# Expert stage of a two-layer decoder: TensorE kept in program order, the next expert's one-hots made on VectorE, one product for a slot's index and weight

## The chip, the cores and the metric

The kernel runs on one core of a Trainium2 chip. The metric is the device time of one execution in microseconds (us).

## What is computed

A trunk of two layers for 512 tokens of width 1024. Each layer mixes tokens by two attention branches and then applies a SwiGLU feed-forward, dense in layer 0 and with experts in layer 1. The change lies in the experts:

```python
def moe_swiglu(h, w_router, w_gu_e, w_dn_e):
    logits = (h @ w_router).astype(jnp.float32)
    top_val, top_idx = lax.top_k(logits, TOP_K)               # 2 of 8
    top_w = jax.nn.softmax(top_val, axis=-1)
    combine = jnp.sum(jax.nn.one_hot(top_idx, N_EXPERTS) * top_w[..., None], axis=-2)
    out = jnp.zeros_like(h)
    for e in range(N_EXPERTS):
        out = out + combine[..., e:e + 1] * swiglu(h, w_gu_e[e], w_dn_e[e])
    return out                                                # D_FF_EXPERT = 1408
```

## The kernel before

**Experts in positions.** Experts are worked on one after the other, at positions e = 0 to 7. Position 0 is always expert 0; the other seven are ranked by how many tokens chose them and taken in the order of the table `ORDER`. An expert takes up to 192 tokens (`CAP`) as slots: 128 rows in the main pass, 64 in an overflow pass that stands in `If` blocks (`over`, L1482) and runs only where more than 128 tokens chose the expert. In the profiled execution that is so at positions 0 and 4.

**Numbers.** A matmul in full precision is made of three on fp32r parts (high by high, high by low, low by high). A weight *piece* (704 KB for gate and up, less for down) is loaded raw by SyncE (`e_load`, L1441), cast to its high part by ScalarE (L1467), and its low part is the difference that VectorE takes (L1468); `e_split` (L1455) issues both. There are 25 pieces to an expert, 16 for gate and up and 9 for down. Eleven raw and nine split pieces can be in memory.

**The stage of one expert** (`expert_blocks`, L1551) is a generator that stops at points (u, k). For u = 0 to 3 it computes 352 columns of gate and of up, over k = 0 to 7 chunks of the width: six matmuls for each k (L1646, L1647), 48 to a u. The overflow rows' 32 matmuls of a u (L1626) use a stationary tile that holds 64 high rows beside 64 low rows; `ov_gu` folds the two halves (a ScalarE copy, a VectorE sum, L1548 and L1549), twice, and multiplies (L1590). For d = 0 to 2, named u = 4 to 6, three matmuls for each of k = 0 to 10 make the down product (L1680 to L1682). It needs the transposed activations `ah` and `al`, which come in groups by `tr` (transposes L1576, ScalarE copy L1580, VectorE difference L1581); the last group is needed from k = 8 of d = 0. `ov_tr` does the same for the overflow rows (L1597, L1600, L1601) and 66 matmuls (L1694, L1695) use its result at the end of d = 0.

**The next expert** is prepared meanwhile, at points that the constants P0, PA, PA1, PA2, PB, PB1 and PO name. `prep_a` (L1485) makes one-hots of the slots, four of 128 by 192, from each token's rank (`one_hots`, L1268); multiplies them with token numbers, 16 products of one column (`slots`, L1278, L1288), and with the three parts of the weights, 8 of three columns (`slot_weights`, L1298, L1306), reads index and weight off, and gathers the rows by an indirect DMA from GpSimd's queue (L1500). `prep_b` (L1517) transposes the gathered rows into `xh` and `xl`; `prep_over` (L1532) does so for overflow rows. `route_rest` (L1206) computes weights, ranks and weight columns during position 0.

**What sets the order.** ScalarE's instructions stand as the program is written. Those of TensorE, VectorE, GpSimd and SyncE are placed by the framework's scheduler at build time; a few are tied by `keep_in_program_order` or a manual dependence. Each engine then runs its own list in order. PSUM tiles come from small rings: two for `py` (all transposes and slot products), four for `pa` (main accumulators), two for `mm` (overflow accumulators).

Of the kernel before, what the change touches and what calls it, by code (L numbers as in the profile page):

```python
# [43 lines left out]
ER = 11  # L44
EA = 4
ORDER = (7, 3, 4, 5, 0, 6, 1, 2)
P0 = (0, 2), (0, 6), (1, 1)
OV, OV3, OT, OY = 5, 6, 8, (5, 8)
ER0 = 3
LA = 2  # L50
SN = (2, 4, 6, 8), (2, 4, 6, 8), (2, 4, 6, 8), (2, 4, 6), (7, 8, 9, 10), (1, 4, 8), (1, 4, 8)
TU, TE = 5, 6
TD = 5
PA, PA1, PA2, PB, PB1, PO = (1, 2), (2, 0), (2, 4), (4, 2), (4, 7), (5, 4)
FD = 3
PINH = ()
BK = 0, 1, 2, 3, 4, 5, 6, 7
# [19 lines left out]
class Trunk:  # L77
# [1128 lines left out]
    def route_rest(self):  # L1206

        nc, rp = self.nc, self.rp

        def over_e(a):  # L1210
            return a.unsqueeze(2).to_broadcast([P, NT, NE])

        e2, w1 = rp.tile([P, NT], F32, name="e2"), rp.tile([P, NT], F32, name="w1")
        nc.vector.tensor_sub(e2, self.m8[:, :, 1], self.m8[:, :, 0])
        nc.scalar.activation(e2, e2, AF.Exp)
        nc.vector.tensor_scalar_add(w1, e2, 1.0)
        nc.vector.reciprocal(w1, w1)
        nc.vector.tensor_mul(e2, w1, e2)
        nc.vector.tensor_sub(self.M, self.M, self.s1)
        nc.vector.tensor_tensor(self.s1, self.s1, over_e(w1), op=ALU.mult)  # L1220
        nc.vector.tensor_tensor(self.M, self.M, over_e(e2), op=ALU.mult)
        nc.vector.tensor_add(self.wt, self.s1, self.M)
        self.rank()
        self.cols = rp.tile([P, NT, NE, 3], BF16, name="cols")
        self.weight_cols(self.cols, self.wtr, rp.tile([P, NT, NE], F32, name="wrem"))

    def rank(self):
# [40 lines left out]
    def one_hots(self, n, pos, q):  # L1268

        oh = []  # L1270
        for t in range(NT):
            o = self.ex.tile([P, CAP], BF16, tag="oh", bufs=4, name=self.nm("oh"))[:, :n]
            i = q.tensor_scalar(o, self.iotas[:, :n], pos[:, t], None, op0=ALU.is_equal)
            self.tc.keep_in_program_order(i)
            oh.append(o)
        return oh

    def slots(self, n, oh):  # L1278

# [205 lines left out]
    def prep_a(self, e):  # L1485

        nc, ex = self.nc, self.ex
        o = ORDER[e]
        oh = self.one_hots(CAP, self.posr[:, :, o:o + 1] if e else self.pos[:, :, 0:1], nc.gpsimd if e else nc.vector)
        yield  # L1490
        sl, fin = self.slots(CAP, oh)
        self.sl = sl
        if e:
            wfin = self.slot_weights(oh, sl, self.cols[:, :, o], self.psl)
            yield
        fin()
        g = self.g = [ex.tile([P, D], F32, tag="xg0", bufs=1, name=self.nm("xg")), self.views[-1]]

        def get(j):
            nc.gpsimd.indirect_dma_start(out=g[j], out_offset=None, in_=self.hd[:, :],  # L1500
                                         in_offset=bass.IndirectOffsetOnAxis(ap=sl[j][2], axis=0))

        get(0)
        if e == 0:
            self.counts()
        self.ne[e] = nc.values_load(self.cnti[0:1, o:o + 1] if e else self.cnti[0:1, NE:], min_val=0, max_val=S)
        with self.over(e):
            get(1)
        if e == 0:
            yield  # L1510
            self.route_rest()
            yield
            wfin = self.slot_weights(oh, sl, self.cols[:, :, o])
            yield
        wfin()

    def prep_b(self):  # L1517

# [32 lines left out]
    def expert_blocks(self, e, sl, xs, xo):  # L1551
# [51 lines left out]
        def ov_y(d):  # L1603
            c = dcol(d)
            self.fold(yo[:, c], ops[d][:, :c.stop - c.start], yo[:, c])
            nc.vector.tensor_scalar_mul(yo[:, c], yo[:, c], sl[1][3])

        def evac_gu(u, pg, pu):
# [8 lines left out]
        last = None  # L1617
        for u in range(DFE // GC):
            ws = self.e_next(KD // GK)
            with self.over(e):  # L1620
                for k in range(KD):
                    hi, lo = ws[k // GK]
                    st, sp, kk = k == 0, k == KD - 1, k % GK
                    for w, s0, s1 in ((hi, st, False), (lo, False, sp)):
                        for g in range(2):
                            nc.tensor.matmul(og[g], xo[:, k], w[:, g, kk], start=s0, stop=s1)  # L1626
            if u:
                evac_gu(u - 1, *last)
            last = pg, pu = self.psa()[:, :GC], self.psa()[:, :GC]
            for k in range(KD):  # L1630
                yield u, k
                if (u, k) == (0, ER0) and self.rest:
                    self.rest()
                if k == OV and u < 3:
                    with self.over(e):
                        ov_gu(u)
                if k == TU:
                    trev = tr(u * GC // P)
# [12 lines left out]
        for d in range(ND):  # L1651
            if d == 0:
                dws.append(self.e_next(3))
            if d != 1:
                py = self.psa()
            pd, py = py[:, :dcol(d).stop - dcol(d).start], None
            for k in range(KE):
                yield 4 + d, k
                if d == 0 and k == TD:
                    tr(KE)()  # L1660
                if k in SN[4 + d]:
                    self.e_split()
                if d == 0 and k == OV3:
                    with self.over(e):
                        ov_gu(3)
                if d == 0 and k == OT:
                    with self.over(e):
                        ov_tr()
                if d and k == 1:
                    evac_y(d - 1, last)  # L1670
                if (4 + d, k) == OY:
                    with self.over(e):
                        for j in range(ND):
                            ov_y(j)
                        nc.gpsimd.indirect_dma_start(out=self.out[0],
                                                     out_offset=bass.IndirectOffsetOnAxis(ap=sl[1][2], axis=0),
                                                     in_=yo, in_offset=None, compute_op=ALU.add)
                hi, lo = dws[d][k // DK]
                kk = k % DK
                nc.tensor.matmul(pd, ah[:, k], hi[:, 0, kk], start=k == 0, stop=False)  # L1680
                nc.tensor.matmul(pd, ah[:, k], lo[:, 0, kk], start=False, stop=False)  # L1681
                nc.tensor.matmul(pd, al[:, k], hi[:, 0, kk], start=False, stop=k == KE - 1)  # L1682
            last = pd
            if d == 0:
                py = self.psa()
                dws += [self.e_next(3) for _ in range(ND - 1)]
                ops.append(self.psa())
                with self.over(e):
                    for j, ws in enumerate(dws):
# [15 lines left out]
    def moe(self):  # L1705
# [19 lines left out]
            self.e_load()  # L1725
        self.hold = False
        next(pb)
        xo = self.prep_over(0)
        self.e_splits(1 + LA)
        for e in range(NE):  # L1730
            sl = self.sl
            for u, k in self.expert_blocks(e, sl, self.xs, xo):
                if e == 0 and (u, k) in P0:
                    next(pa, None)
                if e + 1 == NE:
                    continue
                if (u, k) == PA:
                    pa = self.prep_a(e + 1)
                if (u, k) in (PA, PA1, PA2):
                    next(pa, None)  # L1740
                if (u, k) == PB:
                    pb = self.prep_b()
# [74 lines left out]
    def whole(self):  # L1817
# [14 lines left out]
        with order:  # L1832
# [15 lines left out]
                self.route()  # L1848
            with experts:
                self.moe_pools(experts)  # L1850
                self.moe()
                with tc.issue_after(self.last_dve.ins):
                    self.overflow_list()
        with ExitStack() as experts:
# [29 lines left out]
```

## Time and profile before

| | |
|---|---|
| median of 3 runs | 1703.38 us (1703.5, 1700.21, 1703.38) |
| profiled execution, its own time | 1699.52 us |
| its span | 1697.7 us |
| expert matmuls in it, first and last start | 1198.0 us, 1684.97 us after the span's start |
| position 0 / 4 (with overflow rows) | about 84 / 86 us |
| each other position | about 52 us |

Positions follow each other without a gap on TensorE. The span begins at the first instruction; times of rows are counted from there, and 1.8 us of the profiled execution's own time lie outside it. In a profile's row, `out<-in` are tiles by the program's names, and the bracket at a row's end says how long the engine was idle before it and what released it.

### The profile page before, as it was taken

The numbers are of one execution on the slowest core, as the hardware profiler recorded it, in microseconds if no ns is written. First come the engines' busy times: TensorE is split into PE (matmuls) and PEld (weight loads), VectorE is DVE, ScalarE is ACT, GpSimd is POOL, SyncE is SP. The second block draws the span as 40 slices with busy tenths as digits, with TensorE's granted clock in tenths as the row PEclk, the third lists the DMA queues.
The fourth block names the chain that finished last, engine by engine and source line by source line (L and its number), as shares of the span: only waits on it lengthen the run. The fifth ranks groups of instructions, "written<-read, shape, count | busy, mean of one in ns | idle before, by whom it ended". The sixth has DMA issues, their size and how long they took to land. (4 is left out here: it accounts for less than half of the span.)

```text
span 1697.7 us, 26160 instructions
## 1 busy us (share of the span) xinstructions
PE 1634.0 (96%) x9031; PEld 1425.7 (84%) x9031; DVE 1093.7 (64%) x1844; ACT 977.9 (58%) x1750; POOL 205.5 (12%) x315
## 2 busy tenths in 40 slices
PE   6999999999999999999999999998899999999996
PEld 6878987888888888888878987887889999999996
DVE  5588678666533332336588688655767878767984
ACT  5677589755322222324677589643656776656873
POOL 6122000001000000100122000102012201102200
PEclk9999999999999999999999999999899999999998
DMA  7334332235333332443433233352959899869993
GB/s 181 108 96 116 82 88 71 86 110 165 100 98 99 100 99 84 134 130 100 112 105 107 72 88 78 110 194 95 311 201 331 296 360 351 295 209 336 321 344 87
DMA packets 270840, 273.73 MB, mean 161 GB/s; under 512 B 11424, under 2 KB 259232, under 8 KB 270688
## 3 DMA queue, kind: packets, MB, share of 16 engines
q1 hardware_dynamic: 255936, 230.98, 43.2%
q0 software_dynamic: 12288, 37.40, 8.1%
q10 hardware_dynamic: 2464, 3.41, 0.6%
q8 instruction: 85, 1.39, 0.3%
q14 instruction: 67, 0.55, 0.1%
HBM read 250.21 MB, written 13.14 MB: 155 GB/s over the span
## 5 line engine op out<-in xcount | busy, mean ns | idle before, releaser
L320 PE MATMUL mm<-b,whi 128*128 128x512 f32 x1072 | 426.7, 398 | 3.6 <-DVE b L534 2.7
L322 PE MATMUL mm<-b,wlo 128*128 128x512 f32 x1072 | 419.4, 391 | 0.0
L321 PE MATMUL mm<-b,whi 128*128 128x512 f32 x1072 | 419.4, 391 | 0.0
L297 DVE TENSOR_TENSOR wlo<-wr,whi 128x1024 fp32r<-128x1024 f32 (+1 forms) x176 | 213.3, 1213 | 214.5 <-ACT whi L296 212.5
L296 ACT CAST whi<-wr 128x1024 fp32r<-128x1024 f32 (+1 forms) x176 | 183.2, 1043 | 268.9 <-PE mm L321 121.5
L1468 DVE TENSOR_TENSOR elo<-er,ehi 128x1408 fp32r<-128x1408 f32 (+3 forms) x200 | 305.1, 1569 | 26.0 <-ACT ehi L1467 15.9
L1467 ACT CAST ehi<-er 128x1408 fp32r<-128x1408 f32 (+3 forms) x200 | 256.2, 1324 | 18.7 <-DMA er<-in_w_gu_exp_dram 6.2
L320 PEld LDWEIGHTS mm<-b,whi 128*128 128x128 f32 x1072 | 201.7, 188 | 45.4 <-DVE b L534 4.7
L322 PEld LDWEIGHTS mm<-b,wlo 128*128 128x128 f32 x1072 | 201.3, 188 | 42.8 <-DVE wlo L297 0.4
L321 PEld LDWEIGHTS mm<-b,whi 128*128 128x128 f32 x1072 | 201.7, 188 | 38.5 <-issue 0.2
L356 PE MATMUL mm<-whi,b 128*128 128x256 f32 x320 | 92.0, 288 | 1.8 <-DVE b L532 1.1
L357 PE MATMUL mm<-wlo,b 128*128 128x256 f32 x320 | 91.0, 285 | 0.4 <-DVE wlo L297 0.4
L358 PE MATMUL mm<-whi,b 128*128 128x256 f32 x320 | 90.8, 284 | 0.0
L1681 PE MATMUL pa<-elo,ah 128*128 128x352 f32 (+1 forms) x264 | 85.6, 324 | 2.7
L1682 PE MATMUL pa<-ehi,al 128*128 128x352 f32 (+1 forms) x264 | 84.4, 320 | 3.3 <-DVE al L1581 3.3
L1680 PE MATMUL pa<-ehi,ah 128*128 128x352 f32 (+1 forms) x264 | 86.2, 327 | 0.9
L1647 PE MATMUL pa<-elo,xh 128*128 128x352 f32 x256 | 83.7, 327 | 2.1 <-PEq L1620 0.5
L1646 PE MATMUL pa<-ehi,xh 128*128 128x352 f32 x256 | 85.7, 335 | 0.0
L1647 PE MATMUL pa<-ehi,xl 128*128 128x352 f32 x256 | 83.2, 325 | 0.9
L1646 PE MATMUL pa<-elo,xh 128*128 128x352 f32 x256 | 83.0, 324 | 0.3 <-DVE elo L1468 0.3
L1646 PE MATMUL pa<-ehi,xl 128*128 128x352 f32 x256 | 83.2, 325 | 0.0
L1647 PE MATMUL pa<-ehi,xh 128*128 128x352 f32 x256 | 82.9, 324 | 0.0
(351 smaller groups left out, 3087.7 us busy)
## 6 DMA issues: line engine op xcount, KB each, us to landing
er<-in_w_gu_exp_dram SPq DMA_DIRECT2D x248, 352.0 KB
wr<-in_w_in_dram SPq DMA_DIRECT2D x80, 512.0 KB
wr<-in_w_gu_dense_dram SPq DMA_DIRECT2D x44, 512.0 KB
er<-in_w_dn_exp_dram SPq DMA_DIRECT2D x32, 704.0 KB
wr<-in_w_dn_dense_dram SPq DMA_DIRECT2D x20, 512.0 KB
er<-in_w_dn_exp_dram SPq DMA_DIRECT2D x16, 640.0 KB
er<-in_w_dn_exp_dram SPq DMA_DIRECT2D x16, 528.0 KB
b<-b POOLq DMA_DIRECT2D x64, 128.0 KB, 2.8
```

Of the source, the lines that this page charges most:

```text
L296: self.nc.scalar.copy(hi, raw)
L297: self.nc.vector.tensor_sub(lo, raw, f32v(hi))
L320: self.nc.tensor.matmul(ps, hi[:, j], hh[j], start=st, stop=False)
L321: self.nc.tensor.matmul(ps, hi[:, j], hl[j], start=False, stop=False)
L322: self.nc.tensor.matmul(ps, lo[:, j], hh[j], start=False, stop=sp)
L356: nc.tensor.matmul(o, a, hi[:, j], start=first, stop=False, skip_group_check=True)
L357: nc.tensor.matmul(o, a, lo[:, j], start=False, stop=False, skip_group_check=True)
L358: nc.tensor.matmul(o, b, hi[:, j], start=False, stop=last, skip_group_check=True)
L1467: self.nc.scalar.copy(hi, raw)
L1468: self.last_dve = self.nc.vector.tensor_sub(lo, raw, f32v(hi))
L1646: nc.tensor.matmul(pg, x[:, k], w[:, 0, kk], start=s0, stop=s1)
L1647: nc.tensor.matmul(pu, x[:, k], w[:, 1, kk], start=s0, stop=s1)
```

## The change

- `moe` is traced with TensorE in program order too, so a matmul stands where the generator issues it.
- The one-hots of positions 1 to 7 are made by VectorE, not GpSimd, and at an earlier point: (0, 6) in place of (1, 2), with the products at (1, 5) in place of (2, 0). In position 0 these points are later: (2, 1), (2, 6) and, for the gather, (3, 1).
- The weight columns get two more, the token numbers in two parts (`cols` has 5), copied there by GpSimd once; `slots_all` makes index and weight by one set of 8 products of five columns, in place of 16 and 8.
- In position 0 the overflow rows are prepared inside the loop, at (0, 2), and their first matmuls stand at (0, 4); `route_rest` stands ahead of the loop, the slots' weights at (2, 0) and (2, 2).
- `ov_gu` of the last piece stands at k = 5 of u = 3 like the others' (before: at k = 6 of d = 0), and `ov_tr` at k = 3 of d = 0 (before: 8). That of position 0's first piece stands at k = 7.

```diff
-P0 = (0, 2), (0, 6), (1, 1)
-OV, OV3, OT, OY = 5, 6, 8, (5, 8)
+P0 = (2, 0), (2, 2)
+EO = 2
+OV, OT, OY = 5, 3, (5, 8)
-PA, PA1, PA2, PB, PB1, PO = (1, 2), (2, 0), (2, 4), (4, 2), (4, 7), (5, 4)
+PA = ((2, 1), (2, 6), (3, 1)), ((0, 6), (1, 5), (2, 4))
+PB, PB1, PO = (4, 2), (4, 7), (5, 4)
...
+        self.cols = rp.tile([P, NT, NE, 5], BF16, name="cols")
+        for j in range(2):
+            nc.gpsimd.tensor_copy(self.cols[:, :, :, 3 + j], self.tokc[:, :, j:j + 1].to_broadcast([P, NT, NE]))
...
+    def slots_all(self, n, oh, cols):
...
+            o = ps[:m, (b // P) * 8:(b // P) * 8 + 5]
+            for t in range(NT):
+                nc.tensor.matmul(o, oh[t][:, b:b + m], cols[:, t], start=t == 0, stop=t == NT - 1)
...
+                    nc.vector.tensor_reduce(ix, o[:, 3:5], axis=AX.X, op=ALU.add)
+                nc.vector.tensor_reduce(w, o[:, 0:3], axis=AX.X, op=ALU.add)
...
-        oh = self.one_hots(CAP, self.posr[:, :, o:o + 1] if e else self.pos[:, :, 0:1], nc.gpsimd if e else nc.vector)
+        oh = self.one_hots(CAP, self.posr[:, :, o:o + 1] if e else self.pos[:, :, 0:1], nc.vector)
         yield
-        sl, fin = self.slots(CAP, oh)
+        sl, fin = self.slots_all(CAP, oh, self.cols[:, :, o]) if e else self.slots(CAP, oh)
...
         for u in range(DFE // GC):
             ws = self.e_next(KD // GK)
+            if (e, u) != (0, 0):
+                mm_over()
...
             for k in range(KD):
                 yield u, k
+                if (e, u, k) == (0, 0, EO):
+                    xo = self.prep_over(0)
+                    self.e_splits(LA)
+                if (e, u, k) == (0, 0, EO + 2):
+                    mm_over()
-                if k == OV and u < 3:
+                if k == (OV if e or u else KD - 1):
                     with self.over(e):
                         ov_gu(u)
...
-                if d == 0 and k == OV3:
-                    with self.over(e):
-                        ov_gu(3)
...
-        xo = self.prep_over(0)
-        self.e_splits(1 + LA)
+        xo = None
+        self.e_splits(1)
+        next(pa)
+        p0 = pa
...
-                self.moe()
+                with tc.manual_schedule(engines={mybir.EngineType.PE}):
+                    self.moe()
```

`mm_over` is the block of a u's 32 overflow matmuls, unchanged, now a function.

**What moves on the engines.** Ahead of the expert stage all lists are the same, but for the two copies on GpSimd. TensorE, the slot products for position 1, before (tile `oh` is a one-hot, `tokc` the token numbers, `mm` the overflow accumulators):

```order
L1288 LDWEIGHTS oh_12022
L1288 MATMUL py_12137<-tokc,oh_12022 128x1
L1620 COMPARE_AND_BRANCH
L1626 MATMUL mm_11660<-ehi_11945,aot 128x352
L1626 MATMUL mm_11661<-ehi_11945,aot 128x352
L1626 MATMUL mm_11660<-elo_11946,aot 128x352
L1626 MATMUL mm_11661<-elo_11946,aot 128x352
```

and now:

```order
L1289 LDWEIGHTS oh_12135
L1289 MATMUL py_12210<-cols,oh_12135 128x5
L1289 LDWEIGHTS oh_12137
L1289 MATMUL py_12210<-cols,oh_12137 128x5
L1289 LDWEIGHTS oh_12139
L1289 MATMUL py_12210<-cols,oh_12139 128x5
L1289 LDWEIGHTS oh_12141
L1289 MATMUL py_12210<-cols,oh_12141 128x5
```

Before, the 16 index products were cut by an overflow block and by main matmuls, and 8 weight products followed; now 8 products stand together, ahead of the block, and nothing follows them.

TensorE, the end of d = 0 in position 0, before (`ao` are overflow activations, `aot` their transposes, `al` the low part of the main ones):

```order
L1680 MATMUL pa_12399<-ehi_12337,ah_11801 128x352
L1681 MATMUL pa_12399<-elo_12338,ah_11801 128x352
L1667 COMPARE_AND_BRANCH
L1597 MATMUL py_12468<-ident,ao 128x64 x8
L1597 MATMUL py_12479<-ident,ao 128x64 x3
L1667 UNCONDITIONAL_BRANCH x2
L1682 MATMUL pa_12399<-ehi_12337,al_11802 128x352
L1688 COMPARE_AND_BRANCH
L1694 MATMUL mm_11660<-ehi_12260,aot 128x352
```

and now, nearer to the start of d = 0:

```order
L1696 COMPARE_AND_BRANCH
L1620 MATMUL py_12414<-ident,ao 128x64 x8
L1620 MATMUL py_12425<-ident,ao 128x64 x3
L1696 UNCONDITIONAL_BRANCH x2
L1709 MATMUL pa_12394<-ehi_12226,ah_11820 128x352
L1710 MATMUL pa_12394<-elo_12227,ah_11820 128x352
L1711 MATMUL pa_12394<-ehi_12226,al_11821 128x352
L1709 MATMUL pa_12394<-ehi_12247,ah_11820 128x352
L1710 MATMUL pa_12394<-elo_12248,ah_11820 128x352
L1711 MATMUL pa_12394<-ehi_12247,al_11821 128x352
L1599 MATMUL py_12437<-ident,am 128x128 x3
```

The overflow transposes stood one main matmul ahead of the first matmul that reads `aot`; now they stand behind 9 of the 33 main matmuls, and the last `am` transposes come behind them.

VectorE, the same place, before:

```order
L1529 TENSOR_TENSOR xl_12407<-py_12408,xh_12406 128x512
L1664 COMPARE_AND_BRANCH
L1549 TENSOR_TENSOR ao<-mm_11660,ao 64x352
L1549 TENSOR_TENSOR ao<-mm_11661,ao 64x352
L1590 TENSOR_TENSOR ao<-ao 64x352
L1664 UNCONDITIONAL_BRANCH x2
L1581 TENSOR_TENSOR al_11802<-py_12424,ah_11801 128x384
L1529 TENSOR_TENSOR xl_12407<-py_12443,xh_12406 128x512
L1667 COMPARE_AND_BRANCH
L1601 TENSOR_TENSOR aot<-py_12468,aot 128x8x64
L1601 TENSOR_TENSOR aot<-py_12479,aot 128x3x64
```

and now:

```order
L1613 TENSOR_TENSOR ao<-ao 64x352
L1667 UNCONDITIONAL_BRANCH x2
L1492 TENSOR_TENSOR elo_12375<-er_12011,ehi_12374 128x1408
L1604 TENSOR_TENSOR al_11821<-py_12361,ah_11820 128x384
L1643 TENSOR_TENSOR am<-am,pa_12287 128x352
L1552 TENSOR_TENSOR xl_12402<-py_12403,xh_12401 128x512
L1696 COMPARE_AND_BRANCH
L1624 TENSOR_TENSOR aot<-py_12414,aot 128x8x64
L1624 TENSOR_TENSOR aot<-py_12425,aot 128x3x64
L1696 UNCONDITIONAL_BRANCH x2
L1604 TENSOR_TENSOR al_11821<-py_12437,ah_11820 128x384
```

Before, the three instructions of the last `ov_gu` (`ao`) stood between the first `xl` and the last `al`; now they stand ahead of the first `al`, and the two differences for `aot` have the place before the last `al`.

## Rows read from the trace of the kernel before

**Rows 1.** The page, part 1: busy time, share of the span, instructions.
```profile
PE 1634.0 (96%) x9031; PEld 1425.7 (84%) x9031; DVE 1093.7 (64%) x1844; ACT 977.9 (58%) x1750; POOL 205.5 (12%) x315
```

**Rows 2.** Busy time by engine in two stretches: us, busy (x instructions), clock, DMA share, GB/s.
```profile
1198.00:1282.00 84.00, 79.01 (x506) 75.86 (x505) 56.69 (x88) 49.48 (x60) 6.35 (x6) 0.97 0.81 273
1334.00:1386.00 52.00, 50.64 (x333) 48.64 (x332) 43.19 (x40) 36.92 (x38) 9.70 (x6) 1.00 1.05 351
```

**Rows 3.** TensorE waits, 1198 to 1698 us: us in total, times, longest.
```profile
PE pa L1682 <- DVE al L1581: 3.3, 2, 2.1
PE mm L1694 <- DVE aot L1601: 1.7, 2, 0.9
PE py L1539 <- DMA ao<-hd,ix: 0.7, 1, 0.7
PE py L1288 <- POOL oh L1273: 0.7, 2, 0.5
PE pa L1647 <- PEq L1620: 0.5, 1, 0.5
PE pa L1646 <- DVE elo L1468: 0.3, 1, 0.3
```

**Rows 4.** Timeline, TensorE, position 6: start us, length us, instruction, count.
```profile
1599.91 0.69 PE L1288 MATMUL py<-tokc,oh 128*128 128x1 bf16 x16
1600.54 0.47 PE L1306 MATMUL py<-cols,oh 128*128 128x3 bf16 x8
1600.94 0.43 PE L1646 MATMUL pa<-ehi,xh 128*128 128x352 f32 x1
```

**Rows 5.** Timeline, TensorE, position 0, down stage; idle before it and its releaser.
```profile
1261.65 0.49 PE L1576 MATMUL py<-ident,am 128*128 128x128 f32 x3
1265.49 0.43 PE L1682 MATMUL pa<-ehi,al 128*128 128x352 f32 x1 [2.11 <-DVE al L1581]
1268.84 0.40 PE L1694 MATMUL mm<-ehi,aot 128*128 128x352 f32 x1 [0.95 <-DVE aot L1601]
```

**Rows 6.** Timeline, VectorE, the same stretch.
```profile
1261.17 0.68 DVE L1529 TENSOR_TENSOR xl<-py,xh 128x512 fp32r<-128x512 f32 x1
1263.16 1.07 DVE L1549 TENSOR_TENSOR ao<-mm,ao 64x352 f32<-64x352 f32 x2 [1.30 <-ACT ao L1548]
...
1264.88 0.56 DVE L1581 TENSOR_TENSOR al<-py,ah 128x384 fp32r<-128x384 f32 x1
...
1268.00 0.96 DVE L1601 TENSOR_TENSOR aot<-py,aot 128x512 fp32r<-128x512 f32 x2 [1.97 <-ACT aot L1600]
```

**Rows 7.** Timeline, position 0, first overflow block: TensorE, then ScalarE, then VectorE.
```profile
1206.08 0.48 PE L1626 MATMUL mm<-ehi,aot 128*128 128x352 f32 x2
...
1208.99 1.38 ACT L1467 CAST ehi<-er 128x1408 fp32r<-128x1408 f32 x1 [0.59 <-DMA er<-in_w_gu_exp_dram]
1211.22 0.93 ACT L1548 COPY ao<-mm 64x352 f32<-64x352 f32 x2 [0.85 <-PE mm L1626]
...
1211.70 1.07 DVE L1549 TENSOR_TENSOR ao<-mm,ao 64x352 f32<-64x352 f32 x2 [1.43 <-ACT ao L1548]
```

**Rows 8.** The line of the gathers: time to landing; and the gather of position 1.
```profile
DMA to landing us min/median/max: 4.5/7.6/9.2
...
1243.54 2.35 POOL L1500 DMA_INDIRECT xg<-hd,ix  x1 [5.80 <-DVE w L1312]
```

**Rows 9.** The line of the one-hots: length ns min/median/max, first and last start.
```profile
L1273 POOL TENSOR_SCALAR oh<-iotas,posr x28: 753/1358/3960, 1234.7 to 1594.2; 128x192 bf16<-128x192 f32 x28
...
L1273 DVE TENSOR_SCALAR oh<-iotas,r_pos x4: 299/301/302, 1188.9 to 1189.6; 128x192 bf16<-128x192 f32 x4
```

**Rows 10.** ScalarE waits, 1281 to 1680 us.
```profile
ACT ehi L1467 <- DMA er<-in_w_gu_exp_dram: 4.5, 6, 1.9
```

**Rows 11.** Timeline, the end: TensorE and GpSimd.
```profile
1684.97 0.31 PE L1682 MATMUL pa<-ehi,al 128*128 128x320 f32 x1
...
1686.12 1.56 POOL L1699 DMA_INDIRECT out_dram<-am,ix  x1 [45.61 <-ACTq L1787]
```

More of the change, by code (lines that the diff above doesn't have):

```diff
@@ L1223, in route_rest @@
         self.rank()
-        self.cols = rp.tile([P, NT, NE, 3], BF16, name="cols")
+        self.cols = rp.tile([P, NT, NE, 5], BF16, name="cols")
+        for j in range(2):
+            nc.gpsimd.tensor_copy(self.cols[:, :, :, 3 + j], self.tokc[:, :, j:j + 1].to_broadcast([P, NT, NE]))
         self.weight_cols(self.cols, self.wtr, rp.tile([P, NT, NE], F32, name="wrem"))
@@ L1276, in one_hots, with fin @@
         return oh
+    def slots_all(self, n, oh, cols):
+        nc, ps, res = self.nc, self.psy(), []
+        for b in range(0, n, P):
+            m = min(P, n - b)
+            o = ps[:m, (b // P) * 8:(b // P) * 8 + 5]
+            for t in range(NT):
+                nc.tensor.matmul(o, oh[t][:, b:b + m], cols[:, t], start=t == 0, stop=t == NT - 1)
+            res.append([b, m] + [self.ex.tile([P, 1], d, tag=g, bufs=4, name=self.nm(g))[:m]
+                                 for d, g in ((I32, "ix"), (F32, "w"))])
+        def fin():
+            for b, m, ix, w in res:
+                o = ps[:m, (b // P) * 8:(b // P) * 8 + 5]
+                with nc.allow_low_precision(reason="whole numbers below 512"):
+                    nc.vector.tensor_reduce(ix, o[:, 3:5], axis=AX.X, op=ALU.add)
+                nc.vector.tensor_reduce(w, o[:, 0:3], axis=AX.X, op=ALU.add)
+        return res, fin
     def slots(self, n, oh):
@@ L1512, in prep_a @@
             yield
-            wfin = self.slot_weights(oh, sl, self.cols[:, :, o])
+            wfin = self.slot_weights(oh, sl, self.cols[:, :, o, 0:3])
             yield
-        wfin()
+            wfin()
     def prep_b(self):
@@ L1606, in ov_y, with mm_over @@
             nc.vector.tensor_scalar_mul(yo[:, c], yo[:, c], sl[1][3])
+        def mm_over():
+            with self.over(e):
+                for k in range(KD):
+                    hi, lo = ws[k // GK]
+                    st, sp, kk = k == 0, k == KD - 1, k % GK
+                    for w, s0, s1 in ((hi, st, False), (lo, False, sp)):
+                        for g in range(2):
+                            nc.tensor.matmul(og[g], xo[:, k], w[:, g, kk], start=s0, stop=s1)
         def evac_gu(u, pg, pu):
@@ L1619, in expert_blocks @@
             ws = self.e_next(KD // GK)
-            with self.over(e):
[L1621 to L1626, printed above, removed]
+            if (e, u) != (0, 0):
+                mm_over()
             if u:
@@ L1662, in expert_blocks @@
                     self.e_split()
-                if d == 0 and k == OV3:
-                    with self.over(e):
-                        ov_gu(3)
                 if d == 0 and k == OT:
@@ L1733, in moe @@
                 if e == 0 and (u, k) in P0:
-                    next(pa, None)
+                    next(p0, None)
                 if e + 1 == NE:
                     continue
-                if (u, k) == PA:
+                at = PA[min(e, 1)]
+                if (u, k) == at[0]:
                     pa = self.prep_a(e + 1)
-                if (u, k) in (PA, PA1, PA2):
+                if (u, k) in at:
                     next(pa, None)
```

1 line of the change is left out of this document (removed).

## The prediction

> **What bounds the kernel now.** I read the page's first part first: TensorE is busy for 1634.0 of 1697.7 us [rows 1], no other engine comes near. That is an average over stages, so I next read busy time by stretch. In an expert without overflow rows (1334 to 1386 us) TensorE is busy 50.64 of 52 us at clock 1.00, VectorE 43.19, ScalarE 36.92, GpSimd 9.70; the DMA share is 1.05 at 351 GB/s [rows 2]. So there TensorE sets the time, the weight stream runs close behind, and VectorE has 9 us to spare. In position 0, with overflow rows, VectorE is busy 56.69 of 84 us and the DMA share is 0.81 [rows 2]: the slack is larger, but TensorE idles 5 us. Third I read what TensorE waits for in the whole stage: 7.2 us in all, of it 5.0 for `al` and `aot`, twice each [rows 3]. What can be won is therefore those waits and work taken off TensorE. Ahead of the first expert matmul all lists are the same but for two copies on GpSimd, so everything up to 1198 us stays.
>
> **The change part by part.** I sum against the profiled execution's own 1699.5 us. It is the lowest of four; the median of the runs shown is 1703.4.
>
> *One set of products.* In position 6, 16 index products start at 1599.91, 8 weight products at 1600.54, the next main matmul at 1600.94 [rows 4]: 24 products in 1.03 us, 43 ns each. The change leaves 8, so 16 x 43 ns = 0.69 us go, in each of the 7 preparations: **-4.8 us**. They stand in TensorE's own list, so all of it is on the path. Five columns in place of one or three shouldn't lengthen a product, as three columns went at the pace of one: 8 in 0.40 us, 50 ns, against 16 in 0.63, 40 ns. If the weight product's 50 ns holds for the new one, 0.06 x 7 = 0.4 us less is gained.
> The Trainium skill (TensorE: Matmul & The Clock Gate, "LDWEIGHTS (loading the stationary operand)") gives a weight load columns / 1.2 ns, so 107 ns for the 128-column and 53 ns for the 64-column half of these products; by it, as an estimate, the term would be 9.0 us. The trace disagrees, at 43 ns a product [rows 4], and the measurement decides.
>
> *One-hots on VectorE, earlier.* GpSimd's take 1358 ns in the middle and up to 3960, VectorE's 300 [rows 9]. TensorE's wait for them, 0.7 us in two places of position 0 [rows 3], goes, for they are now made at (2, 1) and used at (2, 6): **-0.7**. VectorE gets 4 x 0.30 = 1.2 us an expert, hidden by its 52 - 43.19 = 8.8 us of slack [rows 2]; without that cover, 7 x 1.2 = 8.4 us. The reduces are fewer in kind and cost nothing more on TensorE's path. GpSimd's two copies to `cols` stand where it has nothing to do.
>
> *Position 0's gathers.* The wait of 0.7 for `ao<-hd,ix` goes [rows 3], as the transposes of the overflow rows now stand at k = 2, behind 12 main matmuls: **-0.7**. The gather for position 1 moves from (2, 4) to (3, 1), five k-steps of six matmuls at 0.16 us, 4.8 us, later. Before, it was issued at 1243.54 [rows 8]; an issue some 5 us later has its rows by 1248.5 + 9.2 = 1258 at the longest landing [rows 8], and its transposes at (4, 2) lead to the first `xl` difference only at 1261.17 [rows 6]. No cost taken; the end of the range carries up to 2 us. From position 2 on the gather comes no later than before.
>
> *Last overflow piece at once.* Before, the three `ao` instructions of `ov_gu`, the first at 1263.16 for 1.07 us each, held VectorE until `al` at 1264.88 [rows 6], and TensorE, ready since the `am` transposes at 1261.65, idled 2.11 us ahead of 1265.49 [rows 5]. The overflow transposes came a matmul ahead of their use, their two differences at 1268.00 [rows 6], and TensorE idled 0.95 us more [rows 5]. Now `ov_gu` ends an eighth of a piece after its matmuls, and 24 main matmuls stand between the transposes of `ao` and their first reader. Both waits go, in both overflowed positions: 3.3 + 1.7 [rows 3] = **-5.0**.
>
> *TensorE in program order.* The wait of 0.3 for `elo` [rows 3] belongs to a matmul the scheduler had pulled ahead: **-0.3**. The branches remain as many, 13 an expert.
>
> *New waits.* (a) In position 0 the first overflow block (0, 4) and the second (u = 1) now have 24 main matmuls between them, about 3.9 us at the 0.16 us of a matmul's pace. The second uses the same two `mm` tiles and waits until `ov_gu(0)` has read them. Before, the first block began at 1206.08, ScalarE got to the copies at 1211.22 behind a cast that waited on a weight DMA, VectorE's sums came from 1211.70 [rows 7]. The block's 32 matmuls last 5.1 us; it now starts about 4 us later, so TensorE is at the second at about 1214; the copies stand behind two casts (1.38 us each, paced by arriving pieces) and may end between 1213 and 1215.6. So 0 to 1.6 us; I take **+0.5**, nearer the casts that come on time. (b) In `ov_tr` two `py` tiles are wanted one after the other, and one of them is the ring's last `xh`/`xl`, freed by a VectorE difference of 0.68 us [rows 6]. It can cost 0 to 0.7 in each of two positions; I take half, **+0.6** together.
>
> Sum: -4.8 - 0.7 - 0.7 - 5.0 - 0.3 + 0.5 + 0.6 = **-10.4 us**, so 1689.1 for that execution. From the median it is 1693.0; between both, nearer the median, I put **1692**. With both new waits at their low ends and nothing lost it is -11.5; with them at their high ends (+1.6, +1.4), the gather's 2 us and the 0.4 of the products it is -6.1.
>
> **The rivals.** *The weight stream is next.* ScalarE already waits 4.5 us for raw pieces in six places [rows 10], and the stream runs at a DMA share of 1.05 [rows 2]. If DMA can give no more, the four positions whose stream is as full as that of rows 2 keep their length: 4 x 0.69 = 2.8 us not gained, so 1695. Against it: pieces arrive ahead of use nearly everywhere, as `elo` holds TensorE once, for 0.3 us [rows 3].
>
> *Program order trades its gain.* With no scheduler to pull main matmuls ahead of a late tile, TensorE meets new stops, in overflowed positions above all: `am` transposes, `aot`, `mm`. If the 5.0 us return as other waits, the gain is 5.4: 1698. For it: a list in program order can't step around a late tile. Against it: six waits in all [rows 3], and the new places give 9 to 24 matmuls of cover.
>
> *Slower: VectorE's list holds the weights.* The index and weight reduces wait for products that TensorE makes in program order, and in VectorE's list they stand ahead of `elo` differences that TensorE needs soon after. VectorE is busy 83% of such a position [rows 2]. It decides once a position's stops and its 1.2 us of one-hots use up the 8.8 idle us, or sooner, where a stop falls just ahead of a piece that is late anyway. If it throws VectorE back by two pieces, each put at the 1.38 us of a cast [rows 7], 2.8 us are lost in each of 7 preparations: 19.3 - 10.4 = +9, 1711. Against it: before, the reduces waited for products too, and TensorE waited for `elo` 0.3 us in all [rows 3].
> The Trainium skill (Perfetto Trace Analysis, "Optimizing Scalar/DVE Operations") advises to move work off VectorE, to GpSimd at most, when VectorE is saturated, the reverse of this edit, and warns that the two share an SBUF port. Here it would bite only if the 83% were as good as full; the trace has VectorE idle 8.8 us an expert [rows 2].
>
> *The change doesn't do what it says.* The lists show 8 products, one-hots on VectorE and `ov_gu` at its new place; only if the waits of rows 3 were caused elsewhere would nothing change: 1702.
>
> **How the numbers follow.** Forecast 0.60; products and waits as summed. Waits traded 0.16, stream 0.12, VectorE's list 0.08, no effect 0.04. About 0.2% (3.4 us) is what a measurement of this kernel can tell from no change; against the median, faster means under 1700. Forecast and stream are faster, of waits traded some 0.11: 0.83. Same: 0.05 of waits traded, 0.04 no effect, 0.02 of VectorE's: 0.11. Slower: 0.06. The range reaches from 1686 (the -11.5 against the profiled execution's time is 1688, and 2 us of spread) to 1701, which takes in stream and traded waits, and leaves VectorE's list out. The tail from the last matmul at 1684.97 over the scatter at 1686.12 [rows 11] to the end, 12.7 us, stays as it is.
>
> **What would show it.** Right: 8 slot products in about 0.4 us where 24 took 1.03, the rows `al`, `aot`, `oh` and `ao` gone from TensorE's waits, position 0 about 5 us and position 4 about 2 us shorter, others 0.7. A wait for `ao` ahead of the second overflow block and one for `xl` at the overflow transposes give (a) and (b) their sizes. Wrong: TensorE waiting for `elo` or for `py` in each position (VectorE's list), a higher ScalarE wait on weight DMA with position lengths kept (stream), or a granted clock below the 1.00 of rows 2 in positions 1 to 7.

## The result, and the profile after

| | before | changed |
|---|---|---|
| median | 1703.16 us (4 runs, 1700.21 to 1703.5) | 1686.51 us (4 runs, 1685.93 to 1688.21) |
| profiled execution, own time / span | 1699.52 / 1697.7 us | 1686.41 / 1684.6 us |

The ratio is 0.9908, interval [0.9891, 0.9925]: 16.7 us less by the medians, 13.1 by the two profiled executions. The forecast was 1692, range 1686 to 1701. The direction was right and the size too small: 10.4 us by the sum. The measured median lies half a microsecond inside the range, and no sum of the terms leads there: with nothing lost they give 1688 from the profiled execution. It is the 2 us put on for spread that took it in, so the hit is in part luck.

The page of the changed kernel, part 1; TensorE is still the bound [rows 1], with 7 us less work:

```profile
PE 1627.1 (97%) x8919; PEld 1420.9 (84%) x8919; DVE 1099.4 (65%) x1872; ACT 977.5 (58%) x1750; POOL 173.5 (10%) x289
```

Busy time by stretch, most of position 0 and position 2, columns as in [rows 2]:

```profile
1198.00:1281.00 83.00, 82.02 (x527) 80.14 (x528) 62.56 (x95) 53.85 (x63) 4.23 (x2) 0.99 0.89 299
1330.00:1382.00 52.00, 50.95 (x323) 48.90 (x322) 44.22 (x45) 37.76 (x39) 4.62 (x2) 1.00 1.05 356
```

In position 2 VectorE took on 1 us and GpSimd gave up 5, and the weight stream runs as fast as it did. TensorE's waits in the whole stage, to be held against [rows 3]:

```profile
PE py L1620 <- DVE xl L1552: 0.7, 2, 0.4
PE pa L1678 <- PEq L1632: 0.5, 3, 0.2
PE mm L1638 <- DVE ao L1572: 0.3, 1, 0.3
PE pa L1709 <- PEq L1696: 0.2, 1, 0.2
```

`al`, `aot`, `oh` and the gather's `ao` are gone. What is left of tiles are the two new waits that the prediction named (a) and (b). The 8 products of position 6 on TensorE's timeline [rows 4]:

```profile
1584.29 0.47 PE L1289 MATMUL py<-cols,oh 128*128 128x5 bf16 x8
1584.69 0.44 PE L1599 MATMUL py<-ident,am 128*128 128x128 f32 x2
```

0.40 us, where 24 had taken 1.03.

**Where the 13.1 us are.** From first expert matmul to first expert matmul: position 0 took 92.13 us before and 85.38 after (6.75 less); positions 1, 2, 3, 5 and 6 lost 0.61, 0.87, 0.57, 0.66 and 0.55 (3.26 together); position 4 2.64; position 7 gained 0.07. The stage starts 0.22 us sooner and the tail is 0.31 shorter; both lie outside the positions, and nothing in the sum stands for them. (Counted so, positions 0 and 4 of the kernel before took 92.13 and 79.40 us, not the 84 and 86 of the table above; the 84 is the stretch of [rows 2], which ends 8 us before position 0 does, and position 4's first overflow block stands in position 3's 57.33.) By the prediction's own terms position 0 should have won 4.6, position 4 2.3, the five others 3.45. So the surplus lies in position 0.

### The profile page after: what moved, and what is told of

Same layout as the page of the kernel before. It is cut to its first block, busy times and chain, and to the rows that moved or that the text cites. A ratio compares the mean times of both kernels' runs of the same rounds, so it can differ in the third digit from the quotient of the medians.

```text
span 1684.6 us, 25937 instructions
## 1 busy us (share of the span) xinstructions
PE 1627.1 (97%) x8919; PEld 1420.9 (84%) x8919; DVE 1099.4 (65%) x1872; ACT 977.5 (58%) x1750; POOL 173.5 (10%) x289
```

## The experiments

Twelve runs follow. Each ratio is to the kernel before on the same chip. *Pitch* is the time from one matmul's start to the next one's.

**1. The changed kernel again.**

> The changed kernel itself, run again beside the variants so that they are compared with it on one chip. Both theories: 1686.5 us, within the 1685.9 to 1688.2 of its four executions; its own spread, about 2 us, is the bound below which no variant of this call can be told from it.

1686.74 us (1685.7 to 1688.42), ratio 0.9910 [0.9896, 0.9924]. The three runs that follow share its chip.

**2. The old products in the changed kernel.**

```diff
-        sl, fin = self.slots_all(CAP, oh, self.cols[:, :, o]) if e else self.slots(CAP, oh)
+        sl, fin = self.slots(CAP, oh)
...
+            wf = self.slot_weights(oh, sl, self.cols[:, :, o, 0:3], self.psl)
```

> The changed kernel with the old products put back: 16 for the index and 8 for the weight, at the place of the 8 joint ones, all else as in the change. Theory (products stand in TensorE's list, which is the bound): 16 x 43 ns x 7 = 4.8 us longer than the changed kernel, 1691.3, and each of positions 0 to 6 about 0.65 us longer. Rival (the weight stream or another engine sets positions 2, 3, 6 and 7 as soon as TensorE gets faster): under 2.5 us longer, the full positions keep their length.

1691.80 us (1690.75 to 1692.32): 5.1 longer, ratio 0.9938. Every gate-and-up stage of positions 1 to 6 is 0.4 to 0.6 us longer, so the weight stream doesn't hide the products. In its rows 24 products take 1.03 us where 8 took 0.40 or 0.41, which makes 4.4 us for seven preparations. That the total comes nearer to 4.8 is in part chance: of the 4.9 us between the profiled executions of runs 1 and 2, 0.9 lie in a later start and a longer tail, which hold no products, and some 0.5 in four more matmuls at the lower clock at the stage's start (run 6).

**3. The last overflow piece and the overflow transposes late again, in program order.**

```diff
-OV, OT, OY = 5, 3, (5, 8)
+OV, OV3, OT, OY = 5, 6, 8, (5, 8)
...
-                if k == (OV if e or u else KD - 1):
+                if k == (OV if e or u else KD - 1) and u < 3:
...
+                if d == 0 and k == OV3:
+                    with self.over(e):
+                        ov_gu(3)
```

> The changed kernel with the last overflow piece folded late again (at k = 6 of the down product's first part) and the overflow transposes at k = 8, in program order. Theory (the waits for al and aot come from that place alone): the two waits return in positions 0 and 4 and the waits of the overflow transposes for xl go; lost pitch before was 2.27 + 1.22 in position 0 and 1.31 + 0.95 in position 4, 5.75 in all, less 0.5 x 2 given back: 4.7 us longer, 1691.2. Rival (program order and the earlier start have already taken these waits away): under 1.5 us longer, no wait of over 0.5 us for al or aot.

1692.37 us (1691.79 to 1693.39): 5.6 longer, ratio 0.9944. TensorE's waits:

```profile
PE py L1620 <- DVE al L1604: 3.1, 2, 1.6
```

The stop returns in another form: the overflow transposes want a `py` tile that the late `al` still holds. The down stages of positions 0 and 4 are 2.65 and 2.83 us longer, 5.5 together. The stops themselves are 3.1 of it. Behind each the granted clock fell to 0.50 (1.2 GHz), and 11 matmuls in each position stand 0.29 us apart in place of 0.16, about 1.4 us each. By stretch, positions 0 and 4:

```profile
1264.00:1266.00 2.00, 2.00 (x8) 2.00 (x8) 2.00 (x4) 2.00 (x2) 0.00 (x0) 0.50 0.05 12
1502.00:1504.00 2.00, 2.00 (x9) 2.00 (x8) 1.45 (x3) 2.00 (x5) 0.00 (x0) 0.50 0.00 0
```

The third number from the right is the granted clock.

**4. No program order on TensorE.**

```diff
-                with tc.manual_schedule(engines={mybir.EngineType.PE}):
-                    self.moe()
+                self.moe()
```

> The changed kernel without the program order on TensorE: the scheduler places its matmuls as before, everything else as changed. Theory (what pays is fewer products and earlier places; order by itself is worth the one wait for elo, 0.5 us of pitch): within 1.5 us of the changed kernel, 1686 to 1688. Rival (program order is what takes the waits away): 4 us longer or more, with waits of TensorE over 0.5 us for al, aot, oh or ao in its rows.

1689.27 us (1688.4 to 1691.06): 2.5 longer, ratio 0.9923, between both expectations. Its waits show a stop that neither kernel had:

```profile
PE py L1599 <- DVE aot L1624: 2.6, 2, 1.3
```

The scheduler puts the last `am` transposes directly behind the overflow transposes, and with two `py` tiles they must wait for `aot`. The down stages of positions 0 and 4 are 1.7 us and 0.7 us longer than in run 1.

**5. The kernel before again.**

> The kernel before, run again, to see what stretches its executions between 1700 and 1704.8 us and the changed kernel's only between 1685.7 and 1688.4. Theory A (the stage's start): the difference of a long and a short execution lies between 1186 and 1206 us, where the clock is at its lower level and TensorE stops for the overflow rows' gather; positions 1 to 7 keep their lengths within 0.3 us. Theory B (the stops in the positions): the waits for al, aot or oh differ by a microsecond or more from execution to execution. Theory C: it lies ahead of the expert stage, in the part that both kernels share, and the changed kernel's executions only happened to be the shorter kind.

1701.41 us over 11 runs (1698.27 to 1704.94), ratio 0.9999 [0.9990, 1.0008]. Its profiled execution (1700.95 us) has the same stops in position 0's down stage, 2.12 us for `al` and 0.58 for `aot`. By stretch:

```profile
1264.00:1266.00 2.00, 0.73 (x4) 0.74 (x5) 1.68 (x3) 1.97 (x3) 0.00 (x0) 1.00 0.22 76
1266.00:1268.00 2.00, 2.00 (x16) 1.46 (x14) 0.09 (x1) 1.55 (x4) 0.00 (x0) 0.71 0.03 8
1268.00:1270.00 2.00, 1.42 (x5) 1.28 (x5) 2.00 (x4) 2.00 (x3) 0.00 (x0) 0.50 0.00 0
1270.00:1272.00 2.00, 2.00 (x8) 2.00 (x8) 2.00 (x3) 0.97 (x2) 0.00 (x0) 0.50 0.37 64
1272.00:1274.00 2.00, 2.00 (x10) 2.00 (x9) 1.91 (x2) 1.00 (x2) 0.00 (x0) 0.58 1.04 343
```

Within two microseconds of the first stop's end (1265.27) the granted clock falls to 0.50, and it comes back at 1273.6. The overflow matmuls in it stand 0.29 us apart in place of 0.16, and this down stage takes 35.16 us; in the first profile, with much the same stops (2.11 and 0.95 us [rows 5]) and the clock at 1.00 throughout, it took 32.81. So the fall is a second price, 2.35 us here, which one execution pays and another doesn't. At the stage's start the two stand the other way round: the first profile stops 0.73 us for the gather [rows 3] and needs 59.32 us for gate and up, the second has no such wait and needs 57.27. Theory A is right on the place, but with the wrong sign: it is the longer execution that lacks the wait at the start. B holds in a form that wasn't foreseen: the waits are alike, their consequence isn't. Positions 1 to 7 are 0.05 to 0.13 us shorter in the second; its stage begins 1.8 us later, so C has a part too.
The Trainium skill (TensorE: Matmul & The Clock Gate, "Part 1: The HAM clock gate") says that the number of matmuls at the lower level varies from run to run of one kernel, that the ramp's penalty is under 1% of a typical span, and that a model shouldn't be fitted to one count. The trace agrees for the stage's start: 12 main matmuls stood at the lower level in the first profile of this kernel, which also had the stop, and 4 in the second. The fall in position 0 is not that ramp, but its 2.35 of 1699 us, 0.14%, are a small share too; here that is a seventh of what was to be explained.

**6. The gather's wait put back at the start.**

```diff
-EO = 2
+EO = 0
```

> The changed kernel with the first overflow rows' transposes at k = 0 of the first piece in place of k = 2, and the block at k = 2: TensorE meets the gather's wait again ahead of any main matmul. Theory (what position 0 won beyond the sum is the clock, which rises 3.6 us earlier since TensorE no longer stops there): a wait of some 2 us for ao, the clock up only at about 1204 us as before, so 2 us longer by the wait and about 1 us more by matmuls at 0.29 in place of 0.16 us: 1689 to 1690. Rival (the clock rises by itself at about 1200 us whatever TensorE does): 1.5 to 2 us longer, clock up at 1200 to 1201.

1688.55 us (1688.11 to 1689.55), ratio 0.9919 [0.9906, 0.9933]: some 1.8 us longer than the changed kernel by the ratios. TensorE's timeline, and the stretch with the clock's rise:

```profile
1202.16 1.09 PE L1562 MATMUL py<-ident,ao 64*128 64x64 f32 x8 [1.98 <-DMA ao<-hd,ix]
```

```profile
1204.00:1206.00 2.00, 2.00 (x10) 2.00 (x9) 2.00 (x2) 1.37 (x1) 0.00 (x0) 0.60 0.98 320
```

For comparison, the same stretch in the changed kernel:

```profile
1200.00:1202.00 2.00, 2.00 (x16) 1.71 (x16) 1.50 (x1) 0.20 (x1) 0.00 (x0) 0.92 1.02 338
```

Counted from the first transposes of the stage (1195.99 and 1198.21), the clock is up after 4.2 us without the stop and after 7 with it; in the first profile of before it was 7.6. So far that agrees with the clock theory, but it doesn't show it, and two things speak against it. The 1 us of slower main matmuls that it expected isn't there: 7 of them stand at 0.29 us here, 8 in the changed kernel. And the clock is also late where TensorE doesn't stop: 5.7 us behind the first transposes in run 2, 9.5 in run 4, 8.0 in run 8. By stretch, run 2, then run 4:

```profile
1200.00:1202.00 2.00, 2.00 (x9) 2.00 (x8) 1.43 (x2) 1.06 (x2) 0.00 (x0) 0.50 0.98 318
```

```profile
1204.00:1206.00 2.00, 2.00 (x8) 2.00 (x8) 1.96 (x4) 0.71 (x1) 0.00 (x0) 0.50 1.00 350
```

What sets the rise is not shown. What run 6 does show is the wait itself, 2.0 us, less the wait (a) of the second block, which is gone here, as the first block comes sooner.

**7. The two new waits taken away.**

```diff
-            if (e, u) != (0, 0):
+            if (e, u) not in ((0, 0), (0, 1)):
...
-                if (e, u, k) == (0, 0, EO + 2):
+                if (e, u, k) in ((0, 0, EO + 2), (0, 1, 2)):
...
-PB, PB1, PO = (4, 2), (4, 7), (5, 4)
+PB, PB1, PO = (4, 1), (4, 7), (5, 4)
```

> The changed kernel with its two new waits taken away: the second overflow block of position 0 at k = 2 of its piece (12 main matmuls ahead of it), and the next rows' first transposes one k earlier, at (4, 1), so that the overflow transposes find a free py tile. Theory: lost pitch 0.48 + 0.39 at the block and 0.51 x 2 at the transposes goes, 1.9 us: 1684.7. Rival (program order only moves the stop to the next late tile): within 0.5 us of the changed kernel.

1685.53 us (1684.94 to 1685.91), ratio 0.9901 [0.9886, 0.9916]. No wait for a tile is left in the stage, and position 0 is 84.42 us long in place of 85.38, position 4 0.23 shorter: 1.2 of the expected 1.9 us. By the ratios it is 0.1% faster than the changed kernel, which is below what can be told.

**8. One edit alone in the kernel before: the last overflow piece and the overflow transposes early.**

```diff
-OV, OV3, OT, OY = 5, 6, 8, (5, 8)
+OV, OT, OY = 5, 3, (5, 8)
...
-                if k == OV and u < 3:
+                if k == OV:
...
-                if d == 0 and k == OV3:
-                    with self.over(e):
-                        ov_gu(3)
```

> The kernel before with one edit of the change alone: the last overflow piece folded at k = 5 of its own block and the overflow transposes at k = 3 of the down product; the scheduler still places TensorE's work. Theory (the stops for al and aot cost their lost pitch, 5.75 us, and in most executions also a fall of the clock, seen from 1267 to 1273 us in the second execution of the kernel before, 2.3 us): the median falls by 5.5 to 8 us, to 1694 to 1696.5, its executions lie closer together (within about 3 us instead of 5 to 6), and the clock stays at 1.00 in positions 0 and 4. Rival (the spread has another cause): 5 us faster at most, with the spread as wide as before.

1700.84 us over 12 runs (1698.31 to 1704.73), ratio 0.9991 [0.9982, 1.0000]. Expected were 5.5 to 8 us; by the ratio the edit alone gives 1.5, between 0 and 3.1. TensorE's timeline in position 0:

```profile
1263.65 0.42 PE L1679 MATMUL pa<-ehi,al 128*128 128x352 f32 x1 [2.33 <-DVE al L1581]
...
1267.16 0.52 PE L1576 MATMUL py<-ident,am 128*128 128x128 f32 x3 [1.31 <-DVE aot L1601]
```

and VectorE's:

```profile
1258.80 4.32 DVE L1468 TENSOR_TENSOR elo<-er,ehi 128x1056 fp32r<-128x1056 f32 x3
1263.04 0.55 DVE L1581 TENSOR_TENSOR al<-py,ah 128x384 fp32r<-128x384 f32 x1
```

The fold (`ao`) no longer stands ahead of `al`, but the scheduler has put three weight differences there, 4.32 us of them; and the second stop is that of run 4. Both stops stay, and so does the spread of 6 us. The clock stayed at 1.00 behind them in this execution.

**9. The one-hots on GpSimd, at the new points.**

```diff
-        oh = self.one_hots(CAP, self.posr[:, :, o:o + 1] if e else self.pos[:, :, 0:1], nc.vector)
+        oh = self.one_hots(CAP, self.posr[:, :, o:o + 1] if e else self.pos[:, :, 0:1], nc.gpsimd if e else nc.vector)
```

> The changed kernel with the one-hots of positions 1 to 7 on GpSimd again, at the new, earlier points. Theory (what took the wait for oh away is the earlier place, and VectorE's share is hidden): within 1 us of the changed kernel, 1686 to 1687.5, no wait for oh in the positions' rows beyond 0.3 us. Rival 1 (GpSimd's four one-hots of 0.75 to 3.96 us each come too late even there): TensorE waits for oh in several preparations, 0.5 us each, 2 to 4 us longer. Rival 2 (VectorE is so full that its relief pays): 1 us or more shorter.

1696.04 us (1694.21 to 1698.69), ratio 0.9961 [0.9947, 0.9976]: 9.5 us longer by the medians. All three expectations were too small. Its waits on TensorE, GpSimd's timeline in position 2, and TensorE's in positions 2 and 6:

```profile
PE py L1289 <- POOL oh L1277: 5.9, 6, 1.7
```

```profile
1339.19 10.40 POOL L1277 TENSOR_SCALAR oh<-iotas,posr 128x192 bf16<-128x192 f32 x4
```

```profile
1348.91 0.18 PE L1289 MATMUL py<-cols,oh 128*128 128x5 bf16 x1 [1.26 <-POOL oh L1277]
...
1593.04 0.18 PE L1289 MATMUL py<-cols,oh 128*128 128x5 bf16 x1 [1.26 <-POOL oh L1277]
```

By stretch, position 2, then position 6:

```profile
1348.00:1350.00 2.00, 0.53 (x7) 0.41 (x7) 0.31 (x1) 0.00 (x0) 1.59 (x2) 1.00 1.06 383
1350.00:1352.00 2.00, 2.00 (x12) 2.00 (x11) 1.91 (x6) 1.55 (x2) 1.47 (x1) 0.68 1.07 363
1352.00:1354.00 2.00, 2.00 (x9) 2.00 (x8) 1.90 (x3) 0.10 (x1) 0.96 (x1) 0.50 1.07 368
...
1594.00:1596.00 2.00, 1.99 (x16) 1.91 (x16) 1.79 (x5) 1.34 (x2) 1.35 (x1) 1.00 1.06 363
```

Four one-hots take 10.4 us on GpSimd and have seven k, 6.7 us, to hide in. TensorE, bound to its order, idles in the 8 products, the clock falls, and 11 matmuls run at 0.29 us: position 2 loses 3.5 us, of it 2.1 in the products and 1.4 (11 x 0.13) to the clock; position 3 loses 4.0. Position 6 has the same two stops, 1.26 and 0.56 us, as position 2, but its clock stays up, and it loses 2.0.

**10, 11. Spare products to keep the clock up at the stage's start.** TensorE idles 5.4 us ahead of the first expert's transposes. 48 products of two constant tiles were put there, in run 11 behind the casts, with the edits of run 7 and `EO = 4`; run 10's place is shown:

```diff
+        for _ in range(48):
+            nc.tensor.matmul(self.ops[0][:, :P], self.onesb, self.identb, start=True, stop=True)
```

> The changed kernel with 48 spare products of 128 columns, whose results nobody reads, in TensorE's idle 5.4 us ahead of the first expert's transposes. Theory (the clock follows what TensorE did in the few microseconds before): it is at 1.00 when the transposes start, 8 transposes at about half their 1.97 us and 8 main matmuls at 0.16 in place of 0.29 us save 1.5 to 2 us: 1684.6 to 1685. Rival (DMA sets this stretch: the pieces land no sooner and TensorE waits for them instead): within 0.5 us of the changed kernel.

1693.02 us, 6.5 longer by the medians and 5.1 by the ratios. ScalarE's timeline of that run:

```profile
1196.74 3.90 ACT L1491 CAST ehi<-er 128x1408 fp32r<-128x1408 f32 x3 [11.23 <-PE mm L1747]
```

> The changed kernel with three edits: the two of the run that mends the new waits; the overflow rows' transposes at k = 4 and the block at k = 6 of the first piece; and the 48 spare products again, now issued behind the first three weight pieces' casts in the program, so that no cast waits for them (in the run with spare products the first cast began at 1196.74 us, 7 us late, released by the spare products). Theory: the clock is up when the first expert's transposes begin, 1.5 to 2 us less than the mended kernel's 1685.5: 1683.5 to 1684. Rival (weights or the gather set this stretch): within 0.5 us of 1685.5.

1688.99 us; the cast is late again, at 1196.67. Issuing it first doesn't help: in the built program the cast waits for a count of TensorE's work, since the piece's buffer takes over the memory of `identb`, which the spare products read. The clock did rise, and fell again, as TensorE then had to wait for `xh` and `xl` (1.9 and 1.3 us in run 10), whose casts stand behind the late ones on ScalarE. By stretch, the run with spare products alone:

```profile
1196.00:1198.00 2.00, 0.70 (x13) 0.53 (x10) 0.00 (x0) 1.26 (x1) 0.00 (x0) 1.00 0.76 219
...
1202.00:1204.00 2.00, 0.72 (x4) 0.51 (x3) 2.00 (x4) 1.11 (x2) 0.00 (x0) 0.66 1.05 333
1204.00:1206.00 2.00, 2.00 (x8) 1.75 (x6) 1.56 (x2) 0.00 (x0) 0.00 (x0) 0.50 1.03 370
```

**12. Run 11 with the cast piece as operand**, and one piece's split moved from k = 2 to k = 4.

```diff
+        hi = self.esplit[0][0]
+        for _ in range(16):
+            nc.tensor.matmul(self.ops[0][:, :GC], hi[:, 0, 0, :P], hi[:, 1, 0], start=True, stop=True)
```

> The mended kernel with the overflow rows' transposes at k = 4 and the block at k = 6 of the first piece, and 16 spare products of the first weight piece with itself in TensorE's idle time ahead of the first expert's transposes. In the two runs with spare products of the constant tiles onesb and identb, the first cast waited for them, as the piece's buffer takes the place of those tiles; the operands are now the cast piece's own, so nothing ahead of the stage can wait for the spare products. Theory (the clock at the stage's start is worth 1.5 to 2 us once nothing stops TensorE after it): clock at 1.00 from about 1196 us on with no fall, first expert matmul within 1 us of the mended kernel's 1198.4, 1683.5 to 1684.5. Rival (the stage's start is set by the gather and the weights, and the clock's lower level costs nothing there): within 0.5 us of the mended kernel's 1685.5. If the clock falls again after it rose, a stop of TensorE between 1196 and 1206 us should stand in the rows.

1684.85 us (1683.26 to 1686.1), ratio 0.9888 [0.9872, 0.9905], on the chip of run 1. By stretch:

```profile
1196.00:1198.00 2.00, 2.00 (x8) 1.57 (x7) 2.00 (x2) 0.00 (x0) 0.00 (x0) 0.50 0.93 361
1198.00:1200.00 2.00, 1.78 (x10) 1.54 (x10) 0.44 (x2) 0.87 (x2) 0.00 (x0) 0.75 1.03 223
1200.00:1202.00 2.00, 2.00 (x13) 1.90 (x13) 1.53 (x3) 1.57 (x3) 0.00 (x0) 1.00 0.94 243
```

The clock is up at 1.00 when the first expert matmul starts (1199.77 in this execution, whose stage began late) and stays. It is the shortest kernel of the study, 1.9 us under run 1 by the medians (0.11%) and 0.22% by the ratios, whose intervals overlap: it can't be told from no change with certainty. It is 0.7 us under run 7 and above the 1683.5 to 1684.5 of its theory, and these times don't part the clock's share from that of run 7's edits.

## Why the prediction was right, and where it was too small

- **One set of products**: 4.8 forecast, 5.1 by run 2, of which the rows give 4.4 to the products, 39 ns for each of the 16. The mechanism held, and the price nearly; five columns cost no more than three.
- **Last overflow piece at once**: 5.0 forecast for the two waits; run 3 gives 5.6. The agreement is partly luck, as run 3 has one stop a position, 3.1 us in all, and two falls of the clock, about 2.9, which the first profile of before doesn't have. And the step laid the gain to the place alone. Run 8 shows that the place without program order is worth 1.5, run 4 that the order is worth 2.5 in the changed kernel. Runs 3, 4 and 8 leave one of the two out each, and all of them have stops here; only with both does none stand for `al` or `aot`.
- **TensorE in program order**, forecast at 0.3, is thereby mis-sized, with run 4's 2.5. The rival "program order trades its gain" fell: TensorE's list stepped into two small stops only.
- **One-hots on VectorE**, forecast at 0.7: that wait is gone. But with GpSimd at the new places it would be 9.5 us (run 9), which the step didn't see. It read GpSimd's cost from a trace where GpSimd had more time. GpSimd's and TensorE's timelines of before, position 2:

```profile
1346.53 7.13 POOL L1273 TENSOR_SCALAR oh<-iotas,posr 128x192 bf16<-128x192 f32 x4
...
1358.63 0.69 PE L1288 MATMUL py<-tokc,oh 128*128 128x1 bf16 x16
```

  There the four one-hots began 12.1 us ahead of the first product and took 7.1; in run 9 they began 8.3 us ahead (1339.19 to 1347.44) and took 10.4.
- **New waits** (a) and (b), forecast at 0.5 and 0.6, stand in the rows with 0.3 and 0.7. Without them (run 7) position 0's gate and up is 0.76 us shorter and the two down stages 0.20 and 0.23, so (a) was worth more than its row and (b) less. Of (a) a part is that the first matmuls behind the stop start slower. TensorE's timeline:

```profile
1213.17 0.95 PE L1638 MATMUL mm<-ehi,aot 128*128 128x352 f32 x2 [0.32 <-DVE ao L1572]
...
1257.03 0.37 PE L1620 MATMUL py<-ident,ao 64*128 64x64 f32 x3 [0.37 <-DVE xl L1552]
```

- **What the sum left out is the pitch around a stop, and the clock.** It priced a stop at the idle time in its row. In position 0, from the first main matmul's start to the 24th's, with the overflow transposes between, 7.60 us passed before and 5.82 after, 1.78 less for a wait put at 0.73. In part that is the clock: 12 matmuls stood at 0.29 us and now 8, and the transposes run at the higher level. The first profile of before, to be held against the changed kernel's stretch in run 6:

```profile
1202.00:1204.00 2.00, 2.00 (x9) 2.00 (x9) 1.42 (x2) 2.00 (x2) 0.00 (x0) 0.53 1.04 347
```

  That the change caused it is not shown: the kernel before itself had 4 such matmuls in run 5, and neither run 5 nor run 8 has the wait of 0.7 for the gather that the sum took off. So both the term and this surplus hang on which execution was profiled. The longer pitch around the other removed stops adds about 0.4 for `al` and `aot`, 0.5 for the products and `oh`, and 0.3 for `elo`; at most half a microsecond of position 0's surplus of 2.1 is left untraced.
- **The 3.6 us between 1699.5 and the median.** The prediction saw them and called the profiled execution the lowest of four. Run 5 shows one part of it, the fall of the clock behind the stops. Of the 26 executions of before on its chip, the five with a mean granted clock of 0.991 or 0.992 took 1698.3 to 1699.8 us, all others 1700.95 to 1704.9. On other chips the two go together less strictly. No execution of 1703 us was profiled, so that this cause makes up all of it stays open.
- **The rivals**: the weight stream did not bind; positions 1, 2, 3, 5 and 6 got shorter by 0.55 to 0.87 us each. ScalarE's waits for gate-and-up weights between 1281 and 1670 us are 1.1 us, against the 4.5 of [rows 10]. VectorE did stop for the products, 4.6 us in three places, the longest 3.1, as the slower rival had it, but TensorE waits for no `elo`: the pieces' lead covers it.

## What to carry to other kernels

Price a stop of a bounding TensorE by the pitch of the matmuls around it, not by the idle time alone, and ask what the clock did afterwards in a second execution: stops of 2.7 us together cost 2.35 more in one of two. Don't lay a difference at the clock to a removed stop before runs without a stop have been looked at, too. A fixed order paid here only together with producers that were early; test such edits in pairs, since each alone may show little or harm. Before giving an engine filler work, look which tile it reads, for another engine may be waiting to reuse that memory.

## What the runs showed of the hardware that was not expected

The clock fell behind stops of 2.12 and 0.58 us (run 5), of 1.56 us (run 3, in both overflowed positions) and of 1.26 and 0.56 us (run 9, position 2). It stayed at 1.00 behind 2.11 and 0.95 us in the first profile of before [rows 5], behind 2.33 and 1.31 us in run 8, and behind 1.26 and 0.56 us in position 6 of run 9. So the length of the stop alone doesn't decide it. Four comparisons of 128x192 that take VectorE 0.31 us each took GpSimd 10.4 us together in position 2 of run 9 and 4.3 us in position 0.
